# One input buffer less, one result buffer more in a batched 64x64 matmul

## The chip, the cores and the metric

The kernel runs on one core of a Trainium2 chip. The metric is the device time of one execution in microseconds (us); the median of several runs is compared. The core has a matmul engine (PE), a vector engine (DVE), a scalar engine (ACT), a general engine (POOL) and a sync engine (SP), which run side by side and wait for one another through semaphores. DMA transfers are issued by SP, ACT and POOL, each on a queue of its own, and all are moved by the core's 16 DMA engines.

## The reference

1024 independent products of 64x64 matrices in f32:

```python
# a: (1024, 64, 64) float32, b: (1024, 64, 64) float32
def reference(a, b):
    return np.matmul(a, b).astype(np.float32)
```

Each of a, b and the result is 16.8 MB. All of it crosses between HBM and the on-chip memory once, 50.3 MB in total. The kernel multiplies in bf16 and accumulates in f32.

## The kernel before

The batch is cut twice. A group *s* is 128 matrices of a (n_s = 8 groups); a tile *t* is 64 products (n_t = 16 tiles), so that group s serves the tiles 2s and 2s+1.

**Input.** `load_a(s)` (line 67) fetches a group of a on POOL's queue in four quarters, each 512 KB in HBM, which the transfer casts to bf16 (256 KB arrive). Group 0 comes in another way: `load_first_a` (line 82) loads its four quarters as f32 on SP's and ACT's queues into the first two buffers of the result pool, which thereby serve twice. `load_b(t)` (line 88) fetches 1 MB of b as f32, on SP's queue for even tiles and on ACT's for odd ones. Four b buffers rotate (`B_AHEAD`).

**From a to a block-diagonal weight.** `regroup(s)` (line 99) is one DVE copy that rearranges the group of a, and after it the a buffer is free. `transpose(s, j)` turns it on PE (line 108), and ACT copies the result out of PSUM (line 111). `spread(t)` (line 121) is four DVE copies into one of two block-diagonal tiles, and `cast(t)` (line 132) is the DVE cast of b to bf16.

**Multiply and evacuate.** `multiply(t)` runs 64 matmuls (line 177) in two halves. Each half is copied from PSUM to the result tile `o_sb` by four copies (line 165): four on ACT for the first half, three on ACT and one on DVE for the second. A result tile is 1 MB and comes from `o_pool`, so the first copy of a tile waits until the store that last used that buffer has landed. `store(t)` (line 154) issues the store on POOL's queue, one tile later than the tile's own turn (`HOLD`). The last two tiles are stored in halves and quarters.

**Order.** The order is written out by hand in the block at the end (`manual_schedule`), and every engine works through its list in that order. One thing is added by the framework: the transfers of POOL use eight completion semaphores in turn, so each transfer on POOL's queue waits, beside what its data needs, for the landing of the one issued eight places before. In the main loop, tile t does spread and cast for t+1, issues `load_b(t+4)`, on even tiles issues `load_a(s + 1 + A_AHEAD)`, multiplies, on even tiles regroups s+2, transposes, and issues the store of tile t-1. So on DVE the regroup of group s+2 stands between the last copy of tile 2s and the spread of tile 2s+2, and on POOL a loads and stores share one list.

The two pools that matter here are the ones with `bufs=A_AHEAD` and `bufs=7`:

Of the kernel before, what the change touches and what calls it, by code (L numbers as in the profile page):

```python
# [13 lines left out]
def kernel(  # L14
# [17 lines left out]
    assert (M, K, N) == (64, 64, 64) and B % 128 == 0  # L32

    n_t, n_s = B // 64, B // 128
    A_AHEAD = 4
    B_AHEAD = 4
    N_BD = 2
    HOLD = 2
# [5 lines left out]
    consts = ctx.enter_context(tc.tile_pool(name="consts", bufs=1))  # L44
    a_pool = ctx.enter_context(tc.tile_pool(name="a_pool", bufs=A_AHEAD))
    b_pool = ctx.enter_context(tc.tile_pool(name="b_pool", bufs=B_AHEAD))
    work = ctx.enter_context(tc.tile_pool(name="work", bufs=2))
    o_pool = ctx.enter_context(tc.tile_pool(name="o_pool", bufs=7))
    t_psum = ctx.enter_context(
        tc.tile_pool(name="t_psum", bufs=4, space=bass.MemoryType.PSUM)  # L50
    )
# [12 lines left out]
    def load_a(s):  # L64
        a_sb = a_pool.tile([128, 4, 16, 64], bf16, name="a_sb")
        for h in range(4):
            nc.gpsimd.dma_start(  # L67
                out=a_sb[:, h, :, :].rearrange("p v k -> p (v k)"), in_=a_v[s, h]
            )
        a_tiles[s] = a_sb  # L70
# [20 lines left out]
    def regroup(s):  # L91
        a_sb = a_tiles.pop(s)
        a_bf = work.tile([128, 16, 4, 64], bf16, name="a_bf")
        if s == 0:
            for h in range(4):
                copy = nc.scalar.copy if h % 2 else nc.vector.tensor_copy
                copy(a_bf[:, :, h, :], a_sb[h].rearrange("p (v k) -> p v k", v=16))  # L97
        else:
            nc.vector.tensor_copy(a_bf[:], a_sb[:].rearrange("p h v k -> p v h k"))  # L99
        abf_tiles[s] = a_bf  # L100
        at_tiles[s] = work.tile([128, 2, 32, 2, 4, 4], fp32, name="at_sb")

    def transpose(s, j):
        a_cols = abf_tiles[s][:].rearrange("p v h k -> p v (h k)").bitcast(fp32)
        for wl in range(2):
            at_ps = t_psum.tile([128, 4, 128], fp32, name="at_ps")
            for vo in range(4):
                nc.tensor.transpose(  # L108
                    at_ps[:, vo, :], a_cols[:, 4 * vo + 2 * j + wl, :], identity[:]
                )  # L110
            nc.scalar.copy(  # L111
                at_tiles[s][:, j, :, wl, :, :],
                at_ps[:].rearrange("p vo (g mp) -> p g mp vo", mp=4),
            )
# [83 lines left out]
    with tc.manual_schedule():  # L198
# [10 lines left out]
        nc.gpsimd.memset(bd_tiles[1][:, 1], 0.0)  # L209
        for s in range(2, A_AHEAD):  # L210
            load_a(s)
# [6 lines left out]
        regroup(1)  # L218
        load_a(A_AHEAD)
        transpose(1, 0)  # L220
        for t in range(n_t):
# [6 lines left out]
            if half == 0:  # L228
                if s + 1 + A_AHEAD < n_s:
                    load_a(s + 1 + A_AHEAD)  # L230
            multiply(t)
# [40 lines left out]
```

## Time and profile before

The median is 136.27 us of five runs (135.78 to 136.86).

| of the profiled execution | |
|---|---|
| its time | 136.09 us |
| span in the trace | 134.3 us |
| DVE busy | 93.7 us (70%) |
| ACT busy | 87.2 us (65%) |
| PE busy | 69.1 us (51%) |
| DMA queue q0 (POOL's): MB, share of 16 engines | 24.12 MB, 62.1% |
| q1 and q10 (the b loads and the first a group): MB, share | 9.44 MB each, 20.1% and 18.7% |
| HBM read and written | 33.55 MB and 16.78 MB |

The page counts a transfer by the bytes at its destination, so a quarter of a counts 256 KB though 512 KB leave HBM. In lines of waits, "X <- Y: 11.8, 2, 6.2" means that X waited for Y 11.8 us in total, twice, 6.2 us at the longest. In a timeline a line begins with start and duration, and ends with the idle time before it and what ended that.

### The profile page before, as it was taken

Reading aid. Unit: us, or ns where it says so; the run is one execution under the profiler, and the core shown is the slowest. Engines: PE = TensorE matmul, PEld = TensorE weight load, DVE = VectorE, ACT = ScalarE, POOL = GpSimd, SP = SyncE. Lnnn points to the kernel's source line nnn. Section 1 sums busy time; section 2 is a strip of 40 time slices with the busy share of each in tenths; the row PEclk is TensorE's granted clock in tenths of the full one; section 3 lists DMA queues with packets and bytes.
Section 4 is the critical chain, followed back from the end, with each engine's and each line's share of the span. In section 5 each row is a group of like instructions: output and inputs, shape, how many; then the busy total and the mean of one; then the engine's idle time right before and its main releaser. Section 6 shows DMA issues by size and latency. Waiting matters only on the chain.

```text
span 134.3 us, 2831 instructions
## 1 busy us (share of the span) xinstructions
PE 69.1 (51%) x1152; PEld 63.9 (48%) x1152; DVE 93.7 (70%) x114; ACT 87.2 (65%) x160; POOL 42.7 (32%) x56
## 2 busy tenths in 40 slices
PE   0006406947396369719554806929183695279000
PEld 0006306945395267619444706829172695279000
DVE  5940359428996998999599903999259987997600
ACT  3135416699479969975995059950899399989300
POOL 8981124113221513340242220732021113035800
PEclk9999975797569986986998695595959559955955
DMA  3999999999999999999999999999999999999991
GB/s 85 364 332 308 308 300 306 310 293 289 307 279 271 292 289 279 287 385 334 290 287 365 399 381 290 257 358 401 398 394 394 393 401 403 400 372 353 328 327 48
DMA packets 17485, 43.18 MB, mean 321 GB/s; under 512 B 1088, under 2 KB 1088, under 8 KB 17472
## 3 DMA queue, kind: packets, MB, share of 16 engines
q0 software_dynamic: 8448, 24.12, 62.1%
q1 hardware_dynamic: 4512, 9.44, 20.1%
q10 hardware_dynamic: 4512, 9.44, 18.7%
q8 instruction: 9, 0.15, 0.4%
q14 instruction: 4, 0.03, 0.1%
HBM read 33.55 MB, written 16.78 MB: 375 GB/s over the span
## 4 chain that ended last, share of the span: by engine, by line
DMA 63%; issue 16%; POOL 11%; ACT 2%; POOLq 1%; ACTq 1%; DVE 1%
DMA a_sb<-in_a_dram 46%; DMA out_dram<-o_sb 17%; POOL out_dram L154 5%; POOL a_sb L67 3%; ACT o_sb L165 2%; POOL at_bd L209 1%; POOL at_bd L207 1%; POOLq L267 1%; DVE o_sb L165 1%; ACTq L88 1%; POOL identity masks.py:199 0%; POOL identity masks.py:197 0%; POOLq L154 0%; POOLq masks.py:199 0%; ACT b_sb L88 0%
## 5 line engine op out<-in xcount | busy, mean ns | idle before, releaser
L165 ACT COPY o_sb<-o_ps 64x512 f32<-64x512 f32 x105 | 61.0, 581 | 22.9 <-DMA out_dram<-o_sb 11.8
L177 PEld LDWEIGHTS <-at_bd 128*128 128x128 bf16 x1024 | 44.7, 116 | 40.4 <-DVE b_bf L132 27.5
L177 PE MATMUL o_ps<-b_bf,at_bd 128*128 128x64 bf16 x960 | 43.6, 218 | 35.2 <-DVE b_bf L132 22.8
L121 DVE COPY at_bd<-at_sb 32x1024 f32<-32x1024 f32 x64 | 47.1, 737 | 7.7 <-ACT at_sb L111 6.0
L154 POOL DMA_DIRECT2D out_dram<-o_sb x20 | 20.3, 1016 | 46.2 <-DVE o_sb L165 24.7
L108 PE MATMUL at_ps<-identity,a_bf 128*128 128x128 f32 x128 | 23.9, 350 | 19.0 <-ACT a_bf L97 11.3
L67 POOL DMA_DIRECT2D a_sb<-in_a_dram x28 | 18.3, 658 | 38.0 <-DMA a_sb<-in_a_dram 31.7
L108 PEld LDWEIGHTS at_ps<-identity,a_bf 128*128 128x128 f32 x128 | 19.8, 185 | 19.8 <-issue 17.9
L165 DVE COPY o_sb<-o_ps 64x512 f32<-64x512 f32 x15 | 10.4, 695 | 18.7 <-ACT o_sb L165 18.5
L111 ACT COPY at_sb<-at_ps 128x512 f32<-128x512 f32 x32 | 17.5, 589 | 3.5 <-PE at_ps L108 3.1
L132 DVE CAST b_bf<-b_sb 128x2048 bf16<-128x2048 f32 x14 | 17.4, 1245 | 0.4
L99 DVE COPY a_bf<-a_sb 128x4096 bf16<-128x4096 bf16 x7 | 8.6, 1227 | 2.3 <-DMA a_sb<-in_a_dram 2.2
L97 ACT CAST a_bf<-o_sb 128x1024 bf16<-128x1024 f32 x2 | 2.1, 1044 | 5.3 <-DMA o_sb<-in_a_dram 5.3
L132 ACT CAST b_bf<-b_sb 128x2048 bf16<-128x2048 f32 x1 | 1.9, 1898 | 4.0 <-DMA b_sb<-in_b_dram 4.0
L97 DVE CAST a_bf<-o_sb 128x1024 bf16<-128x1024 f32 x2 | 3.0, 1502 | 1.8 <-DMA o_sb<-in_a_dram 1.8
L205 DVE MEMSET at_bd<- 128x4096 f32 x1 | 3.5, 3472 | 0.8 <-issue 0.8
L177 PE MATMUL at_ps<-b_bf,at_bd 128*128 128x64 bf16 x64 | 3.6, 242 | 0.8 <-DVE at_bd L121 0.8
L165 DVE COPY o_sb<-at_ps 64x256 f32<-64x256 f32 x8 | 3.4, 422 | 0.1
L165 ACT COPY o_sb<-at_ps 64x256 f32<-64x256 f32 x8 | 2.9, 367 | 0.1
L202 ACT ACT_TABLE_LOAD x1 | 1.3, 1283 | 2.3 <-issue 2.3
L209 POOL MEMSET at_bd<- 128x2048 f32 x1 | 1.9, 1867 | 0.0
L207 POOL MEMSET at_bd<- 128x2048 f32 x1 | 1.8, 1799 | 0.0
(11 smaller groups left out, 3.5 us busy)
## 6 DMA issues: line engine op xcount, KB each, us to landing
out_dram<-o_sb POOLq DMA_DIRECT2D x14, 1024.0 KB, 23.2
a_sb<-in_a_dram POOLq DMA_DIRECT2D x28, 256.0 KB, 20.1
o_sb<-in_a_dram ACTq DMA_DIRECT2D x2, 512.0 KB, 7.4
o_sb<-in_a_dram SPq DMA_DIRECT2D x2, 512.0 KB, 6.2
out_dram<-o_sb POOLq DMA_DIRECT2D x2, 512.0 KB, 7.3
out_dram<-o_sb POOLq DMA_DIRECT2D x4, 256.0 KB, 6.5
b_sb<-in_b_dram SPq DMA_DIRECT2D x8, 0.5 KB, 15.2
b_sb<-in_b_dram ACTq DMA_DIRECT2D x8, 0.5 KB, 14.9
```

The lines of the kernel that those rows point to most:

```text
L67: nc.gpsimd.dma_start(out=a_sb[:, h, :, :].rearrange("p v k -> p (v k)"), in_=a_v[s, h])
L97: copy(a_bf[:, :, h, :], a_sb[h].rearrange("p (v k) -> p v k", v=16))
L99: nc.vector.tensor_copy(a_bf[:], a_sb[:].rearrange("p h v k -> p v h k"))
L108: nc.tensor.transpose(at_ps[:, vo, :], a_cols[:, 4 * vo + 2 * j + wl, :], identity[:])
L111: nc.scalar.copy(at_tiles[s][:, j, :, wl, :, :], at_ps[:].rearrange("p vo (g mp) -> p g mp vo", mp=4),)
L121: nc.vector.tensor_copy(bd[rows, :, :, :, h, :].rearrange("p j g wl mo -> p j (g wl) mo"), at_tiles[t // 2][rows, :, half, :, :, :].rearrange(
L132: (nc.vector.tensor_copy if t else nc.scalar.copy)(b_bf[:], b_sb[:])
L154: nc.gpsimd.dma_start(out=o_v[t, :, lo : lo + n, :], in_=o_sb[:, lo : lo + n].rearrange("p gh j wl n -> p (gh j wl n)"),)
L165: copies[2 * par + wl](dst, src)
L177: nc.tensor.matmul(o_ps[:, gl, g % 2, j, :], at_bd[:, j, g, :, u], b_bf[:, g, 64 * u : 64 * u + 64], start=(u == 0), stop=(u == 1),)
L205: nc.vector.memset(bd_tiles[0][:], 0.0)
L209: nc.gpsimd.memset(bd_tiles[1][:, 1], 0.0)
```

## The change

The pool of a buffers goes from four to three, and the pool of result buffers from seven to eight. Both kinds take 8 KB in each partition, so the memory used is the same. `A_AHEAD` also sets how far ahead a is issued: `load_a(3)` moves from the opening to the place after `regroup(1)`, where `load_a(4)` stood, and in the main loop every a load is issued one even tile later. The instruction lists of PE, DVE, ACT and SP keep their order, and that of POOL changes in the places of the a loads among the stores.

```diff
-    A_AHEAD = 4
+    A_AHEAD = 3
@@
-    o_pool = ctx.enter_context(tc.tile_pool(name="o_pool", bufs=7))
+    o_pool = ctx.enter_context(tc.tile_pool(name="o_pool", bufs=8))
```

## The prediction

> **What bounds the kernel now.** I read the slices first, then the DMA queues stage by stage, then the waits, and last the timelines of ACT and POOL around the longest waits. The page's slices, and the DMA view of 12 to 30 us (its columns: packets, MB at the destination, share of 16 engines):
>
> ```profile
> DMA  3999999999999999999999999999999999999991
> GB/s 85 364 332 308 308 300 306 310 293 289 307 279 271 292 289 279 287 385 334 290 287 365 399 381 290 257 358 401 398 394 394 393 401 403 400 372 353 328 327 48
> ...
> HBM read 33.55 MB, written 16.78 MB: 375 GB/s over the span
> ```
> ```profile
> DMA packets 2845, 5.48 MB, mean 305 GB/s; under 512 B 175, under 2 KB 175, under 8 KB 2844
> ...
> q0 software_dynamic: 966, 1.75, 51.4%
> q1 hardware_dynamic: 961, 1.90, 30.7%
> q10 hardware_dynamic: 917, 1.81, 26.0%
> ```
>
> The DMA engines are full from the second slice to the end, while no compute engine is. The varying GB/s mislead: an a load reads f32 and writes bf16, so it counts half. With the missing half put back, 12 to 30 us moves 305 + 1.75 MB/18 us = 402 GB/s of HBM traffic, 30 to 54 us 286 + 2.69/24 = 398, and 108 to 118 us, stores alone, 402. So in every mix the transfers run at about 400 GB/s, and their order doesn't matter to the total. Only the end is worse: 317 GB/s from 118 to 132.5 us. The bound is 50.33 MB at 400 GB/s (125.8 us), plus 2.2 us before the first data packet, some 3 us lost at the end (14.5 us at 317 instead of 400), which makes 131.0 against a last packet that ends at 132.4, and then what stands outside: the profiled run took 136.09 us for a span of 134.3, and the median of five is 136.27.
>
> The waits, and the two places where ACT stands on a result buffer:
>
> ```profile
> POOL a_sb L67 <- DMA a_sb<-in_a_dram: 31.7, 17, 2.3
> ACT o_sb L165 <- DMA out_dram<-o_sb: 11.8, 2, 6.2
> DVE a_bf L99 <- DMA a_sb<-in_a_dram: 2.2, 2, 1.4
> ```
> ```profile
> 78.65 2.96 ACT L165 COPY o_sb<-o_ps 64x512 f32<-64x512 f32 x5 [6.25 <-DMA out_dram<-o_sb]
> 94.59 2.96 ACT L165 COPY o_sb<-o_ps 64x512 f32<-64x512 f32 x5 [5.56 <-DMA out_dram<-o_sb]
> ```
> ```profile
> 126.80 0.72 POOL L154 DMA_DIRECT2D out_dram<-o_sb  x1 [0.33 <-DVE o_sb L165]
> ```
>
> ACT loses 11.8 us to stores that have not landed, at tiles t=8 and t=10. But the last store is issued at 126.80 and lands at 132.8, behind 2.1 MB of queued stores: compute is ahead of the DMA at the end even with these stalls. I put that lead at about 3 us: the last quarter store alone would need some 0.7 us on POOL, 0.8 us for 256 KB at 317 GB/s and perhaps 1.5 us of latency, and so would land near 129.8.
>
> **What the skill says.** "DMA: Bandwidth & Descriptors", Queues, rings and completion order: an engine goes round the queues that have work, a packet at a time. The view above agrees: 966, 961 and 917 packets. Under "Issuing engines are not separate DMA queues" the page says that all issuers share the same 16 engines; here the three queues' shares sum to about the whole. Under "Anatomy of one DMA" it says that waits are served on the issuing sequencer, never in a DMA engine; POOL's 31.7 us of waiting ahead of a loads agrees, and it means that a POOL issue that waits blocks everything behind it. "HBM Reference", Specifications, gives about 425 GB/s for a core alone; this kernel holds 400, so there is little rate to win.
>
> **The change part by part.** The number of instructions doesn't change on any engine, nor their order on PE, DVE, ACT and SP; SBUF use is equal (8 KB a partition leaves one pool and enters the other). Two things move.
>
> First, POOL's list. Its first sixteen transfers (a1 to a4, four quarters each) stay in order. a4 now needs the buffer of a1, read by the regroup that ends at 21.0, and POOL reaches it at 22.67: no cost. After that the order a5, s0, a6, s1, s2, a7, s3, s4 (s is a store) becomes s0, a5, s1, s2, a6, s3, s4, a7: every later a load falls behind one or two stores of 1 MB. From s5 on the lists agree. Each POOL issue also waits for the transfer eight places before it, so this queue runs as a FIFO that stays several transfers deep. Landing times in the trace of before: a4 50.2, a5 59.2, s0 64.1, a6 74.1, s1 78.6, s2 83.1, a7 91.0, s3 94.5, s4 98.6. The same transfers permuted, each with its own duration (s0 4.95, s1 4.46, s2 4.55, s3 3.49, s4 4.08), give: s0 55.2, a5 64.1, s1 68.6, s2 73.1, a6 83.1, s3 86.6, s4 90.7, a7 98.6. The stores are ready in time: tiles 0 to 4 are evacuated at 29.7, 36.5, 42.7, 48.9 and 54.3, all before their turn. So a5, a6 and a7 arrive 5, 9 and 7.6 us later, and the queue behind them is unmoved.
>
> Second, the result buffers. Two go first to the raw quarters of a0; so before, tile t waits for store t-7, after, for store t-8. Tile 8 waits for s0 (55.2) instead of s1 (78.6), tile 10 for s2 (73.1) instead of s3 (94.5). Both ACT waits go, worth up to 11.8 us on ACT.
>
> Where the stall goes: DVE regroups a5 at 66.9 (a5 lands 64.1, lead 2.8 us, no cost). Tile 8's first half is multiplied from 72.2, so without the wait ACT copies from about 74 to 78.2 and DVE ends tile 8 at 79 instead of 83.5. The next instruction on DVE is the regroup of a6, and a6 lands at 83.1: DVE waits 4 us and starts at 83.3, where it started at 83.55 before. Behind it queue the spread and cast of tile 10, and PE and ACT wait for those. Tile 10: its matmuls start at 89.7, ACT copies from 91.3 instead of 94.6, DVE ends at about 96 instead of 99.45, then waits 3 us for a7 (98.6) and regroups at 98.9 instead of 99.49. From that regroup to the end of compute before took 126.5 - 99.5 = 27.0 us, nearly all work; after, compute ends at 125.9. That is 0.6 us earlier, and buys nothing, because the stores behind it end when the bytes are through.
>
> A correction: b13 and b15 are issued on ACT's queue during tiles 8 and 10, at 81.2 and 97.1 before and some 3 to 4 us sooner after. With one packet in three or four, each can take about 0.5 to 0.6 MB from the a group then under way, up to 1.4 us: a6 at 84.5, which the wait for a7 swallows, and a7 at 100.0, compute ends at 127.3, still inside the lead. The sum: -11.8 us of waits on ACT, some 7 us of new waits on DVE ahead of line 99, the rest hidden, zero on the DMA. 136.09 + 0 in the profiled run's terms, 136.3 for the median.
>
> Unknown costs. Reads, casts and stores now share the engines from 50 to 98 us, before from 59 to 91. Mixed stretches in the trace ran at 390 to 400 GB/s: 16 more us at the low end cost 0.4 us; at the high end nothing. I take 0. The slow end (317 GB/s) I can't explain. If it comes a fixed time after the last b load (110.8) and b15 is 3 us sooner, it costs 3 us x 20% = 0.6 us; if it depends on what is queued it may shrink, to -3 us at best. I take 0 and keep both.
>
> **The rivals.** *A late a7 makes compute the end, slower.* The cover is the 3 us at the end. It is gone when a7 lands after 132.8 - 3.3 - 27.3 = 102.2, that is 3.6 us later than the ledger; from there each us counts in full. For it: a7 is the last thing in its group, and b14 and b15 may run ahead of it. Against: at most 1.4 us of that is found. With a7 at 104, the time is 138.1.
>
> *Mixing costs rate, slower.* Some 0.4 us from the mix and 0.6 us at the end: 137.3. The nearly even 400 GB/s speaks against it.
>
> *The freed ACT pulls in the end, faster.* If the two waits were the bound, up to 11.8 us would go; the full DMA row speaks against it. What stores moved forward could win is the slow end: all of it gives 133.3, half 134.8.
>
> *Nothing changes because the waits don't move.* Then the ACT waits would still be there; the time is 136.3 again.
>
> **How the numbers follow.** About 0.5%, 0.7 us, can be told from no change here. The likeliest case, 136.3 with its own range 135.6 to 137.0, gets 0.59, the case of unmoved waits within it 0.02. Rate lost to mixing gets 0.15, a late a7 0.11, faster 0.15. So faster 0.15, same 0.59, slower 0.26. For eight in ten, the range goes from 135.1, leaving out the better half of the faster case, to 137.9, where a late a7 begins to show fully.
>
> **What would show it.** Right: DMA slices full throughout; the ACT wait on stores gone from the list; "DVE a_bf L99 <- DMA a_sb" grown from 2.2 us to some 7; the last regroup near 99; q0's last landing near 132.8. Wrong: a slice of DMA under 9 between 10 and 125 us; the last regroup after 102; POOL's last store issued after 130; or the rate from 118 us on far from 317 GB/s.

## The result and the profile after

The changed kernel takes 136.94 us in the median (136.04 to 137.39), the kernel before 136.25 us in the runs beside it; the ratio is 1.0046 with a 95% interval of 1.0034 to 1.0059. That is a loss of 0.6 us, real, and just inside the half per cent that the prediction called "same". The profiled execution took 136.69 us for a span of 134.9 us, against 136.09 and 134.3.

The slices of the page after, DMA share and GB/s at the destination:

```profile
DMA  3999999999999999999999999999999999999991
GB/s 87 368 327 310 308 299 305 311 290 286 310 271 255 299 392 310 275 304 391 386 360 308 278 341 394 387 330 256 317 380 397 403 407 403 364 345 333 323 327 63
```

The DMA engines are as full as before. The 400 near the end stands in slices 31 to 34 (the last b load runs beside the stores until 107 us, after it there are stores alone) and falls in slice 35, at about 115 us; before, the fall is in slice 36, near 118 us.

The waits of the kernel after that answer to those shown of before:

```profile
POOL a_sb L67 <- DMA a_sb<-in_a_dram: 27.8, 15, 3.3
DVE a_bf L99 <- DMA a_sb<-in_a_dram: 11.2, 4, 4.9
```

ACT's wait on stores has left the list. DVE's wait for a has come in its place, 2.2 to 11.2 us, and two waits of it are the new ones, in DVE's timeline after:

```profile
82.38 1.23 DVE L99 COPY a_bf<-a_sb 128x4096 bf16<-128x4096 bf16 x1 [2.72 <-DMA a_sb<-in_a_dram]
...
99.69 1.23 DVE L99 COPY a_bf<-a_sb 128x4096 bf16<-128x4096 bf16 x1 [4.86 <-DMA a_sb<-in_a_dram]
```

Before, these two regroups started at 83.55 and 99.49: the stall has changed its engine and not its place. The last store is issued 0.4 us later and lands at 133.4 instead of 132.8:

```profile
127.19 0.72 POOL L154 DMA_DIRECT2D out_dram<-o_sb  x1 [0.33 <-DVE o_sb L165]
```

Where the 0.6 us went shows when HBM bytes are added up packet by packet in the two traces (a packet of a counts with the f32 that it reads). At 116 us the kernel before has moved 44.95 MB and the changed one 44.92; at 90, 100 and 110 us they are equal within 0.2 us of traffic. At 126 us it is 48.55 against 48.33 MB, 0.55 us behind. Nearly all of the loss arises between 114 and 126 us, where only stores run. The DMA view of 112 to 118 us, first before, then after:

```profile
DMA packets 619, 2.40 MB, mean 400 GB/s; under 512 B 36, under 2 KB 36, under 8 KB 618
```
```profile
DMA packets 590, 2.29 MB, mean 382 GB/s; under 512 B 34, under 2 KB 34, under 8 KB 589
```

And from 118 to 124 us, in the same order:

```profile
DMA packets 559, 2.16 MB, mean 360 GB/s; under 512 B 32, under 2 KB 32, under 8 KB 559
```
```profile
DMA packets 533, 2.05 MB, mean 341 GB/s; under 512 B 33, under 2 KB 33, under 8 KB 533
```

From 124 to 130 us it is 331 against 325 GB/s. With 400 GB/s as the measure, the three windows make 0.27 + 0.29 + 0.09 = 0.65 us. In the fast stretch nearly every store packet of 4 KB takes 165 ns. In the slow one the share of longer packets grows: before, 46% are above 172 ns from 118 to 124 us (mean 184 ns), and 87% from 124 to 130 us (mean 197 ns). The slow stretch (more than a quarter of the store packets above 172 ns) begins at 118.0 us before and at 114.75 after; the last b packet starts at 110.1 before and at 107.0 after.

### The profile page after: what moved, and what is told of

The parts are those of the page before. It is cut to its first block, busy times and chain, and to the rows that moved or that the text cites. A ratio compares the mean times of both kernels' runs of the same rounds, so it can differ in the third digit from the quotient of the medians.

```text
span 134.9 us, 2831 instructions
## 1 busy us (share of the span) xinstructions
PE 66.6 (49%) x1152; PEld 61.1 (45%) x1152; DVE 91.5 (68%) x114; ACT 87.3 (65%) x160; POOL 42.3 (31%) x56
## 4 chain that ended last, share of the span: by engine, by line
DMA 51%; issue 20%; POOL 11%; DVE 11%; POOLq 1%; ACT 0%; ACTq 0%; DVEq 0%
DMA a_sb<-in_a_dram 51%; DVE at_bd L121 7%; POOL out_dram L154 5%; DVE b_bf L132 3%; POOL a_sb L67 3%; POOL at_bd L209 2%; POOL at_bd L207 1%; DVE o_sb L165 1%; POOLq L267 1%; ACTq L88 0%; ACT o_sb L165 0%; DVE a_bf L99 0%; POOL identity masks.py:199 0%; POOL identity masks.py:197 0%; POOLq L154 0%
## 5 line engine op out<-in xcount | busy, mean ns | idle before, releaser
L177 PEld LDWEIGHTS <-at_bd 128*128 128x128 bf16 x1024 | 42.7, 113 | 33.0 <-DVE b_bf L132 27.8
L177 PE MATMUL o_ps<-b_bf,at_bd 128*128 128x64 bf16 x960 | 42.4, 215 | 28.4 <-DVE b_bf L132 24.4
L121 DVE COPY at_bd<-at_sb 32x1024 f32<-32x1024 f32 x64 | 46.4, 725 | 7.9 <-ACT at_sb L111 6.2
L108 PE MATMUL at_ps<-identity,a_bf 128*128 128x128 f32 x128 | 23.0, 340 | 28.1 <-ACT a_bf L97 11.2
L154 POOL DMA_DIRECT2D out_dram<-o_sb x20 | 18.9, 944 | 43.1 <-DVE at_bd L121 15.5
L108 PEld LDWEIGHTS at_ps<-identity,a_bf 128*128 128x128 f32 x128 | 19.0, 179 | 29.1 <-issue 17.8
L67 POOL DMA_DIRECT2D a_sb<-in_a_dram x28 | 18.8, 678 | 41.8 <-DMA a_sb<-in_a_dram 27.8
L99 DVE COPY a_bf<-a_sb 128x4096 bf16<-128x4096 bf16 x7 | 8.6, 1227 | 11.2 <-DMA a_sb<-in_a_dram 11.2
L97 DVE CAST a_bf<-o_sb 128x1024 bf16<-128x1024 f32 x2 | 1.5, 771 | 3.0 <-DMA o_sb<-in_a_dram 3.0
L177 PE MATMUL at_ps<-b_bf,at_bd 128*128 128x64 bf16 x64 | 2.9, 221 | 0.3 <-DVE at_bd L121 0.3
L209 POOL MEMSET at_bd<- 128x2048 f32 x1 | 2.4, 2355 | 0.0
L207 POOL MEMSET at_bd<- 128x2048 f32 x1 | 1.8, 1800 | 0.0
```

The source lines that it names most:

```text
L67: nc.gpsimd.dma_start(out=a_sb[:, h, :, :].rearrange("p v k -> p (v k)"), in_=a_v[s, h])
L108: nc.tensor.transpose(at_ps[:, vo, :], a_cols[:, 4 * vo + 2 * j + wl, :], identity[:])
L121: nc.vector.tensor_copy(bd[rows, :, :, :, h, :].rearrange("p j g wl mo -> p j (g wl) mo"), at_tiles[t // 2][rows, :, half, :, :, :].rearrange(
L154: nc.gpsimd.dma_start(out=o_v[t, :, lo : lo + n, :], in_=o_sb[:, lo : lo + n].rearrange("p gh j wl n -> p (gh j wl n)"),)
L177: nc.tensor.matmul(o_ps[:, gl, g % 2, j, :], at_bd[:, j, g, :, u], b_bf[:, g, 64 * u : 64 * u + 64], start=(u == 0), stop=(u == 1),)
```

## The experiments

Three theories stood against one another. *End theory*: stores slow down some time after the b loads have ended, and whatever ends these sooner costs time. *Mixing theory*: a loads that lie longer beside stores cost rate. *Late-compute theory*: the last store waits for the last tile.

**The two halves of the change alone.** First three a buffers with seven result buffers:

```diff
-    A_AHEAD = 4
+    A_AHEAD = 3
```

> Three a buffers, seven result buffers: the first half of the change alone. End theory (the stores slow down some 7 us after the last b load has landed, and the time follows that landing): the a loads lie in the queue as in the changed kernel, so the last b load ends near 107 us, the slow stretch begins near 114.5, ratio to before 1.003 to 1.006. Mixing theory (a loads longer beside stores cost rate): the same 1.004 to 1.005, but with bytes falling behind before 110 us. Late-compute theory (the last store waits for the last tile): 1.003 to 1.005 only if compute ends 0.4 us later than before.

Measured: 136.89 us, ratio 1.0058 (1.0038 to 1.0079). The last b packet starts at 108.1, the slow stretch begins at 115.75 us. The smaller a pool alone costs as much as the whole change; before 110 us its bytes are, if anything, 0.2 us ahead of those of the kernel before, and compute ends 1.2 us sooner than there. Mixing and late compute both fail here. Not all of the loss is slow stores, though: from 110 to 130 us the bytes fall back by 0.4 us, and another 0.4 us goes in the last 4 us, where the 16 engines run out of packets one after another (their mean idle time there is 1.5 us, in the kernel before 1.1). Over all traces of the full kernel this uneven ending takes 0.4 to 2.1 us, and what sets it was not found.

Then four a buffers with eight result buffers:

```diff
-    o_pool = ctx.enter_context(tc.tile_pool(name="o_pool", bufs=7))
+    o_pool = ctx.enter_context(tc.tile_pool(name="o_pool", bufs=8))
```

> Four a buffers, eight result buffers: the second half of the change alone. ACT's wait at tiles 8 and 10 goes, a7 lands as before at about 91 to 93, so compute and the b loads run ahead. End theory: the last b load ends near 101 to 104, the slow stretch begins at 108 to 111, and the time grows by 7 to 10 us x 17% = 1.2 to 1.7 us, ratio 1.008 to 1.012. Mixing theory: the order of a loads and stores is that of before, ratio 1.000. Late-compute theory: compute ends 3 to 5 us earlier, ratio 1.000 or below.

Measured: 137.32 us, ratio 1.0090 (1.0069 to 1.0112). This is the run that tells most. It frees ACT as was hoped, its wait on stores shrinks to one:

```profile
ACT o_sb L165 <- DMA out_dram<-o_sb: 3.4, 1, 3.4
```

Compute ends 6 us sooner, as DVE's copies of the last tile show (duration, then the starts of the first and the last), first before, then in this kernel:

```profile
L165 DVE COPY o_sb<-at_ps x8: 417/422/428, 123.0 to 126.1; 64x256 f32<-64x256 f32 x8
```
```profile
L165 DVE COPY o_sb<-at_ps x8: 417/422/428, 116.7 to 119.8; 64x256 f32<-64x256 f32 x8
```

Yet the kernel is slower, and the b loads end sooner too, at 104.9. The DMA view of the same 112 to 118 us:

```profile
DMA packets 564, 2.18 MB, mean 364 GB/s; under 512 B 31, under 2 KB 31, under 8 KB 564
```

The slow stretch begins at 112.25 us. The two halves don't add up: both together cost less than the second alone. With both, b15 is issued at 92.9 and its last packet starts at 107.0; with the second alone, at 90.9 and 104.9.

**The b loads sooner, nothing else.** The kernel before with a fifth b buffer:

```diff
-    B_AHEAD = 4
+    B_AHEAD = 5
@@
         load_b(3)
+        load_b(4)
         spread(0)
```

> The kernel before with five b buffers, and with them every b load from the fifth on one tile earlier; a loads and stores keep their order. End theory: the last b packets move from 109 to about 103 to 105, the slow stretch begins at 112 to 114 instead of 118, 0.7 to 1.0 us more, ratio 1.004 to 1.009. Mixing theory (a loads beside stores cost rate): a order unchanged, ratio 1.000. Late-compute theory: b is never later, ratio 1.000 or below.

Measured: 137.20 us, ratio 1.0073 (1.0054 to 1.0093). The last b packet starts at 105.3, the slow stretch at 111.25, 112 to 118 us runs at 360 GB/s. In this kernel the last copy on DVE also starts 1.5 us later (127.6), so late compute is not excluded by this run alone; in the kernel with four and eight buffers it is, with compute 6 us ahead.

**The last b load much later.** Issued in tile 13 instead of tile 11, in the changed kernel and in the one before:

```diff
-            if t + B_AHEAD < n_t:
+            if t + B_AHEAD < n_t - 1:
                 load_b(t + B_AHEAD)
+            if t == 13:
+                load_b(n_t - 1)
```

> The changed kernel with the last b load (b15) issued two tiles later, in tile 13. End theory: the last b load ends near 117 to 119, so the slow stretch begins near 124 or never, which saves 6 to 10 us x 17% = 1.0 to 1.6 us against the changed kernel unless the late cast of b15 makes compute the end; ratio to before 0.993 to 0.998. Mixing theory: the a loads are untouched, ratio 1.004 to 1.005. Late-compute theory: the cast of b15 is some 2 us later and so is the last store, ratio 1.010 to 1.020.

> The kernel before with b15 issued in tile 13. End theory: the last b load ends near 117 to 119 instead of 110, the slow stretch begins 6 us or more later, 0.7 to 1.2 us less, ratio 0.990 to 0.996. Mixing theory: ratio 1.000. Late-compute theory: the cast of b15 is some 2 us later, ratio 1.010 to 1.015.

Measured: 140.26 us, ratio 1.0313 (1.0286 to 1.0340), and 140.42 us, ratio 1.0311 (1.0280 to 1.0342). Both miss the end theory's figure, because the load was too late for its cast. The wait of ACT for b15 in the changed kernel:

```profile
ACT b_bf L139 <- DMA b_sb<-in_b_dram: 9.0, 1, 9.0
```

The load was issued at 109.2 and its first packets ran only at 114 us, so the stall was 9 us instead of the 2 that I had reckoned, and the stores ran dry. But the two traces say more about the slow stretch than the times do. With hardly a load packet from 100 us on, stores slowed at 108.25 us and 108.5 us, six to ten us sooner than in their parent kernels and after fewer stored bytes (9.6 MB, in the parents 10.9 and 12.2), and within one to four us of b15's first packets they became fast again. The DMA views of the changed kernel with b15 in tile 13, at 108.5 to 113.5 us and at 117 to 122 us:

```profile
DMA packets 455, 1.76 MB, mean 352 GB/s; under 512 B 25, under 2 KB 25, under 8 KB 455
...
q0 software_dynamic: 455, 1.76, 101.9%
```
```profile
DMA packets 682, 1.99 MB, mean 398 GB/s; under 512 B 32, under 2 KB 32, under 8 KB 682
...
q0 software_dynamic: 344, 1.32, 67.9%
q10 hardware_dynamic: 338, 0.67, 35.0%
```

So the slow stretch doesn't belong to the last tiles, their small stores, an amount stored, or a place in memory. It follows stretches of stores without loads, and a load stream ends it.

**Stores alone, small reads, one tile later.** The kernel with stores only keeps the result pool, fills four tiles with zeros and stores them sixteen times.

> No loads, no products: only the sixteen 1 MB stores of a memset tile, on POOL's queue, through the same view of the result. Write-run theory (stores run at 400 GB/s for 7.7 us without a read beside them and at about 325 GB/s after): packets of 165 ns for the first 7 to 8 us, 190 ns and more after it, the whole in 8 + 13.6 MB/0.325 = 50 us. Drift or end-of-queue theory (the slow stretch belongs to the last tiles and their small stores): about 165 ns and 400 GB/s until the last microseconds, the whole in 42 us.

Measured: one execution, 61.67 us with a span of 59.9; both expectations fail. Every full microsecond of stores ran slow, the first too, at about 200 ns a packet. The windows of that kernel, DVE, POOL, clock, DMA share and GB/s:

```profile
8.00:20.00 12.00, 0.00 (x0) 6.03 (x7) 1.00 1.00 323
20.00:32.00 12.00, 0.00 (x0) 3.54 (x4) 1.00 1.01 330
```

The 330 GB/s is what this stream of stores holds by itself. That kernel has no compute and its stores wait for no data, but the two kernels with b15 in tile 13 show the same with the real stores: their stores stood still for 3 us (126.4 to 129.3 us in one, 126.5 to 129.5 in the other), and the next 128 packets took 188 ns in the mean, though the slow stretch that these two had earlier may have its share in that. The 400 GB/s for the first microseconds after the b loads is the exception, and I read it as left over from the mixed stretch before.

Then four small unused reads at the ends of tiles 12 to 15, in both kernels:

```diff
+            if t >= n_t - 4:
+                nc.scalar.dma_start(out=extra[:, t % 4, :], in_=b_v[0][:, 0, :])
```

> The changed kernel with four reads of 64 KB from b, never used, issued on ACT's queue at the ends of tiles 12 to 15, at about 109, 115, 121 and 125 us. Write-run theory: each read ends the run of pure stores, no slow stretch before 125 or none at all, 8 to 17 us x 17% less 0.65 us for the extra bytes: 0.7 to 2.3 us faster than the changed kernel, ratio to before 0.987 to 0.999. Drift theory (the 16 engines lose step once the b loads end): 4 KB for each engine changes nothing, 0.65 us slower than the changed kernel, ratio 1.008 to 1.011.

> The kernel before with the same four unused reads of 64 KB. Write-run theory: the slow stretch from 118 us goes or shrinks, ratio 0.987 to 0.997, and the difference between the two kernels goes too. Drift theory: 0.65 us more, ratio 1.004 to 1.006.

Measured: 136.72 us, ratio 1.0057 (1.0035 to 1.0079), and 136.27 us, ratio 1.0024 (1.0008 to 1.0039). Both theories' figures are missed in both kernels. In the changed kernel the reads were late: issued at 109.9 and 113.2, they sent their first packet at 114.2, when the slow stretch began (114.25). (Its traced execution, 137.76 us, was also the slowest of eight.) In the kernel before, the first two reads ran from 112.5 to 114.1 and from 117.9 to 120.1 us, and the slow stretch began at 120.0, 2 us later than without. Had each read ended the run of stores, the count would have begun anew at 114.1, and again at 120.1, with no slow stretch before 122; "each read ends the run" fails here. From 124 to 130 us both kernels ran at about 350 instead of 330 GB/s, and the reads paid for about half of their own 0.65 us or more.

And b15 one tile later, in the kernel before:

```diff
+            if t == 12:
+                load_b(n_t - 1)
```

> The kernel before with b15 issued one tile later, in tile 12. Write-run theory: the last b load ends near 113 to 115, in time for its cast at 116 to 120, the slow stretch begins near 121 to 122, 3 to 4 us x 17% = 0.5 to 0.7 us less, ratio 0.994 to 0.997. Mixing theory: 1.000. Late-compute theory: 1.000 while the cast isn't late, more if it is.

Measured: 135.97 us, ratio 0.9988 (0.9977 to 0.9999), a small gain and short of the expected 0.994 to 0.997. The last b packet started at 115.5 but the slow stretch at 117.75, two microseconds later and not eight: b14 had ended at 100, so the stores had already run alone from 100 to 107 us. (The traced execution, 136.41 us, was the slowest of 22.) I added up, in the packet records of the thirteen traces of the full kernel, the time in which the stores ran alone after 90 us (the small reads left out): the slow stretch first began after 8 to 12 us of it, whether it came in one piece (9 us in the changed kernel) or in two or three with loads between them. The 12 is the kernel before with the small reads; with the reads counted as loads it is 9. So a megabyte of b between two such stretches doesn't seem to set the count back to nothing. This count was made after the fact; no run was built to test it.

**The reads kept going without a gap.** b14 and b15 each one tile later, both on ACT's queue, in both kernels:

```diff
-        queue = nc.scalar if t % 2 else nc.sync
+        queue = nc.scalar if t % 2 or t == 14 else nc.sync
@@
-            if t + B_AHEAD < n_t:
+            if t + B_AHEAD < n_t - 2:
                 load_b(t + B_AHEAD)
+            if t in (11, 12):
+                load_b(t + 3)
```

> The kernel before with b14 and b15 each one tile later, both on ACT's queue, so that b packets flow without a gap until about 113. End theory: the slow stretch begins at 121 to 123 instead of 118, 0.5 to 0.8 us less, ratio 0.994 to 0.997. Mixing theory: 1.000. Late-compute theory: 1.000, more if the cast of b14 or b15 is late.

> The changed kernel with b14 and b15 later in the same way. End theory: with the last b packets at about 112 to 114, as in the same edit of the kernel before, the changed kernel's loss of 0.6 us goes: ratio 0.994 to 0.998, within 0.3% of that other. Mixing theory: the loss stays, 1.004 to 1.005. Late-compute theory: the loss stays, 1.004 or more.

Measured in the kernel before: 136.10 us, ratio 1.0016 (0.9998 to 1.0033), no gain. ACT, which now issues b14, stood on a store until 93.9 us there, so b14 went out at 96.5 and the stores ran alone from 92 to 101; they were slow for the first time from 100 to 103 us, and again from 120.5, only 2.3 us after the last b packet had started. b15's packets ended at 118.3, its cast waited 3.3 us, and the last store was issued at 128.67. The bytes were 0.1 us ahead at 124 us, but then the stores ran dry for a moment near 126 us. This is the 1.000 of the rivals and not the end theory's figure: what the rate might have given, late compute took.

Measured in the changed kernel: 134.97 us, ratio 0.9907 (0.9886 to 0.9927), faster than both kernels and beyond what was expected. Here no store holds up ACT, b14 goes out at 93.2 and b15 at 99.0, and b packets run to 113.8 us with hardly a gap. The DMA view of 112 to 118 us in this kernel:

```profile
DMA packets 669, 2.42 MB, mean 403 GB/s; under 512 B 50, under 2 KB 50, under 8 KB 669
```

The slow stretch begins at 122.0 us; 118 to 124 us runs at 392 GB/s where the kernel before has 360 and the changed kernel 341. a7, which no b load overtakes now, is regrouped at 96.5 instead of 99.7, and compute ends 3 us sooner.

**The same with four a buffers.** b14 in tile 11 and b15 in tile 13, four a buffers and eight result buffers:

```diff
+            if t in (11, 13):
+                load_b(14 if t == 11 else 15)
```

> Four a buffers, eight result buffers, b14 issued in tile 11 and b15 in tile 13, both on ACT's queue. Compute of the kernel with four and eight buffers ends near 120 us and can lend some microseconds to a late b15. End theory: b packets flow until about 112, the slow stretch begins at 120 to 122, the cast of b15 waits some 2 to 3 us, which is covered; the loss of that kernel (1.009) turns into a gain, ratio 0.989 to 0.994. Mixing theory and late-compute theory: 1.000, since the a loads lie as in the kernel before and compute ends no later.

Measured: 135.73 us, ratio 0.9971 (0.9958 to 0.9985). The 1.0090 of its parent has become a gain, as the end theory says and neither rival, but the size is missed. b15, issued at 102.3 on a queue whose packets were nearly through, moved almost nothing for four microseconds, as the DMA view of 102.3 to 106.3 us shows:

```profile
q0 software_dynamic: 420, 1.61, 102.0%
q10 hardware_dynamic: 3, 0.00, 0.3%
```

Such a gap is not special to this kernel: b15 of the kernel before, issued at 97.1 on an emptied queue, sent its first packets at 101.1. The stores ran alone for 5 us here, the slow stretch began at 117.75 us, and the cast of b15 waited 7.9 us instead of 2 to 3.

## Why the prediction was right, and what it missed

*The bound.* Right, and shown by the bytes: up to 116 us the kernels move the same amount to within 0.2 us, in a different order.

*The permuted queue.* Right. a5, a6 and a7 were put at 64.1, 83.1 and 98.6 (100.0 with b15 in the way); they landed at 63.8, 82.2 and 99.7. s3 and s4 were put at 86.6 and 90.7, and landed at 87.3 and 91.3.

*The stall that moves.* Right in place, under in size. The regroups of a6 and a7 were put at 83.3 and 98.9 and started at 82.4 and 99.7; the waits ahead of them are 2.7 and 4.9 us, 7.6 together for the 7 foretold. The wait for a grew to 11.2 us in total and not to 7: the foretold figure left out the two waits early in the kernel, 2.2 us before and 3.6 after, of which the later one stands at 31.8 us, ahead of every transfer that moved.

*Compute and the lead at the end.* Compute was put at 125.9 to 127.3 and ended at 126.9. The lead of about 3 us fits. In the two kernels with b15 in tile 13, whose stores had run dry, the last store took 3.3 us from issue to landing, part of it still behind the store ahead; in the changed kernel it took 6.2 us (127.19 to 133.4). So at least 2.9 us of that was lead. Two readings on the way were loose: of the 2.1 MB of "queued stores", which had not landed at the last issue, 1.5 MB were still to be moved; and 108 to 118 us is not stores alone from its start, since b15's packets ran to 110.1.

*The slow end.* This is the term that was mis-sized. The prediction named it and priced it: if the slow stretch came a fixed time after the last b load and b15 were 3 us sooner, 0.6 us. It then took 0. b15 was issued 4.2 us sooner (92.9 instead of 97.1), its packets ended 3.1 us sooner, the slow stretch came 3.25 us sooner, and the cost was 0.6 us. What I counted against a7 (b15 runs ahead of it) was the smaller effect of that earlier issue; the larger one was that the loads ended earlier. The other half of "rate lost to mixing", 0.4 us for a loads beside stores, did not show: no bytes were behind before 114 us.

*The rivals.* A late a7 did not decide: with three and seven buffers compute ended 1.2 us sooner than before and the loss was the same. The faster case failed, and its reason is the opposite of what it said. It held that stores moved forward and a freed ACT could only win at the end; with four and eight buffers a freed ACT lost 1.2 us there.

So 136.94 us lies in the likeliest case's own range, but only just (its upper end is 137.0, its centre 136.3). "No change" was right as a bracket; the change is in truth a small loss with a cause that can be turned around.

What stays open is why stores slow down. The runs show when: after 8 to 12 us of stores without loads, summed over pieces; at once in the kernel that had nothing but stores; and not any more after some microseconds of a full load stream. Whether this lies in the memory or in how the 16 engines fall in with one another was not settled.

## What to carry to other kernels

In this kernel, whose DMA is full from start to end, the buffer counts only permuted the transfers, and the prediction was a permutation of the landing times. In such a case look at what the order does to the mix: a kernel that prefetches its inputs as early as its buffers allow ends on a stretch of pure stores, and here that stretch was the only one after the start that ran far below 400 GB/s. The Trainium skill says under "Perfetto Trace Analysis", Optimization Strategy, that a kernel whose most-contended engine changes over time may gain by interleaving those regimes. Here the DMA engines were the most contended throughout, and only their mix of loads and stores changed; interleaving helped there too: holding the last two loads back until just before they were needed turned a loss of 0.5% into a gain of 0.9%, as long as the loads ran without a gap and the cast was not late. The same edit gave nothing in the kernel before (1.0016), where both conditions failed.

## What the runs showed of the hardware that was not expected

- Stores of 1 MB alone held 323 to 333 GB/s (packets of 4 KB at about 200 ns). Stores and loads together, and stores for some 9 us after the loads, held about 400 GB/s (store packets at 165 to 169 ns).
- A b load issued on a queue that had run empty or nearly so, while the other queues kept the engines full, sent its first packets 3.9 to 4.9 us after its issue, beside stores (109.2 to 114.0 us, b15 in tile 13) as beside loads (92.9 to 97.2 us, the changed kernel). Two loads in a row on one queue had no such gap.
- An earlier end of compute, by 6 us, went with a slower kernel, because the same freedom let the loads end sooner.
